# Turning the last query block's probabilities with 32x32 transposes and copies in the second attention of a two-layer trunk

## The chip, the cores and the metric

The kernel runs on one core of a Trainium2 chip. The metric is device time in microseconds (us) of one execution, the median of several. A core has a matrix engine (TensorE, PE in the profile; PEld are its weight loads), a vector engine (VectorE, DVE), an activation engine (ScalarE, ACT), a general engine (GpSimd, POOL) and an engine that issues transfers (SyncE, SP). They run side by side, each in its own order, and wait for one another at semaphores. Operands lie in SBUF, 128 partitions wide; TensorE writes to PSUM, which has eight banks of 128 x 512 float32 values.

## The reference

Two layers on 512 tokens of 1024 values. Each has an attention of 16 heads of 64 values and a gated MLP with 2816 inner values. The first layer's attention is stick-breaking; the second's, with which this document deals, is a softmax with a decay:

```python
z = jnp.einsum('bhqd,bhkd->bhqk', qb, kb).astype(jnp.float32) * scale
decay = cum[:, :, q0:k_end, None] - cum[:, :, None, :k_end]
logits = jnp.where(s_idx <= t_idx, z + decay, -jnp.inf)
p = jax.nn.softmax(logits, axis=-1)
outs.append(jnp.einsum('bhqk,bhkd->bhqd', p.astype(vb.dtype), vb))
```

Queries are taken in blocks of 128. Block 0 sees 128 keys, block 3 all 512. So a head has ten 128x128 blocks of probabilities, four of them in the last query block.

## The kernel before

Weights are loaded in tiles of 128x1024 and split on the chip into a rounded high half (ACT, L270) and a low half (POOL or DVE, L271); every product with a weight is three matmuls (`mm3`, L344 to L346). Three tiles of each half are kept, and a stream `ws` loads two tiles ahead of the one in use.

`attention` (L597) goes over the heads. For head h it issues the scores of query blocks 3, 2, 1, 0 (`scores`, L466, two matmuls each). In the second layer `fox` (L481) makes probabilities of each block: DVE adds the decay and finds the extreme value (L487), ACT takes the exponential and its sum (L490), DVE takes the reciprocal (L491) and scales (L492). The result `fx` has queries on partitions and keys along the row.

For the products with v the keys must be on partitions. This is done one head late: when head h has issued its block 2, `transposed` (L495) turns the probabilities of head h - 1. TensorE transposes 128x128 blocks into PSUM (tile `pa`, L504), and ACT evicts each bank to a tile `at` (L507). Three banks are used: key block 0 (512 columns, from four query blocks), key blocks 1 and 3 (384 and 128), and key block 2 (256). When both heads of a pair are turned, `weighted` (L510) multiplies them with v: for each key block and head one matmul of F32 operands (L516), into the pair's half of the 128 partitions of bank `po`, with the columns from that key block's first query to 511. The result is split into `oh` and `ol`, from which the output projection reads.

Between these steps, `fill` runs pieces of other work on TensorE: projections of later heads (`pqk`), values (`pv`), and towards the end the output projection of early heads. How many pieces each head gets is written in `UNITS`.

The orders of TensorE and of the transfer queue are those of the program. ACT, DVE and POOL are ordered by a planner, which goes by estimated costs; on the chip each then runs in that fixed order. Most 128x512 tiles (probabilities, `at`, v, queries and keys, `oh` and `ol`, some weights) share 44 slots of one pool; a new tile waits for a free one.

Of the kernel before, what the change touches and what calls it, by code (L numbers as in the profile page):

```python
# [8 lines left out]
F32 = mybir.dt.float32  # L9
F32R = mybir.dt.float32r  # L10
# [5 lines left out]
P = 128  # L16
D = 1024
S = 512
NT = S // P
ND = D // P  # L20
NH = 16
HD = 64
# [8 lines left out]
RES = 4  # L31
UNITS = [[10, 10, 10, 11, 10, 9, 10, 11, 9, 10, 10, 12, 8, 10, 4, 9, 6],
         [18, 12, 12, 12, 12, 12, 13, 12, 12, 12, 11, 9, 10, 10, 4, 9, 5]]
SH_A, SC_A, GT_A, SH_F, SC_F, GT_F = range(6)


@with_exitstack
def trunk(ctx, tc, x, c, w_mod, b_mod, g_mix_pre, g_mix_post, w_qkv, w_o, w_fg, b_fg,
          g_ffn_pre, g_ffn_post, w_gate, w_up, w_conv, b_conv, w_down, out):
    nc = tc.nc  # L40
    cst = ctx.enter_context(tc.tile_pool(name="cst", bufs=1))
# [5 lines left out]
    def nm(s):  # L47
        serial[0] += 1
        return f"{s}_{serial[0]}"

    def bank(s="b"):
        return pp.tile([P, 512], F32, tag="bank", name=nm(s), bufs=8)

    def slot(s, dt=F32R):
        return sb.tile([P, 512], dt, tag="slot", name=nm(s), bufs=NS)
# [17 lines left out]
    make_identity(nc, idn)  # L73
    onesf = cst.tile([P, P], F32, name="onesf")
    nc.vector.memset(onesf, 1.0)
    ones = cst.tile([P, P], F32R, name="ones")
    nc.vector.tensor_copy(ones, onesf)
    mhalf = cst.tile([P, 1], F32, name="mhalf")
    nc.vector.memset(mhalf, -0.5)
    mask = cst.tile([P, P], F32, name="mask")  # L80
# [188 lines left out]
    def split(hi, lo, src, engine=None):  # L269
        nc.scalar.copy(hi, src)  # L270
        (engine or nc.vector).tensor_tensor(lo, src, hi.bitcast(F32), op=ALU.subtract)  # L271
# [189 lines left out]
    def scores(l, hd, qb, q, k):  # L461
        n = (qb + 1) * P
        qs = slice(qb * P, n)
        ps = bank("ps")
        for i in range(2):
            nc.tensor.matmul(ps[:, :n], q[hd][:, qs], k[hd][i][:, :n], start=i == 0, stop=i == 1)  # L466
        return ps, n

    def stick(ps, n):


        bt = slot("bt", F32)
        om = slot("om", F32) if n > MULN else ps
        nc.gpsimd.memset(bt[:, n - 1 : n], 0.0)
        nc.scalar.activation(bt[:, : n - 1], ps[:, : n - 1], AF.Sigmoid)
        nc.scalar.activation(ps[:, :n], ps[:, :n], AF.Sigmoid, scale=-1.0)
        nc.vector.tensor_tensor_scan(om[:, :n][:, ::-1], ps[:, :n][:, ::-1], zid[:, S - n :][:, ::-1], 0.0, op0=ALU.mult, op1=ALU.add)
        (nc.gpsimd if n > MULN else nc.vector).tensor_tensor(bt[:, : n - 1], bt[:, : n - 1], om[:, 1:n], op=ALU.mult)
        return bt

    def fox(ps, qb, cum):  # L481

        n = (qb + 1) * P
        t = slot("fx", F32)[:, :n]
        e = t if n > MULN else ps[:, :n]
        m, s, r = tiny("mx"), tiny("sm"), tiny("rc")
        nc.vector.tensor_tensor_reduce(  # L487
            e.rearrange("p (b k) -> p b k", k=P), ps[:, :n].rearrange("p (b k) -> p b k", k=P), cum(qb),
            1.0, BIG, op0=ALU.add, op1=ALU.min, accum_out=m)
        nc.scalar.activation(e, e, AF.Exp, scale=-1.0, bias=m, accum_out=s)  # L490
        nc.vector.reciprocal(r, s)  # L491
        nc.vector.tensor_scalar(t, e, r, None, op0=ALU.mult)  # L492
        return t

    def transposed(probs):  # L495

        res = {}
        for kbs in ((0,), (1, 3), (2,)):
            ps, t, o = bank("pa"), slot("at", F32), 0
            for kb in kbs:  # L500
                n = (NT - kb) * P
                for qb in range(NT - 1, kb - 1, -1):
                    c = o + (qb - kb) * P
                    nc.tensor.transpose(ps[:, c : c + P], probs[qb][:, kb * P : (kb + 1) * P], idn)  # L504
                res[kb] = t[:, o : o + n]
                o += n
            nc.scalar.copy(t[:, :o], ps[:, :o])  # L507
        return res

    def weighted(p, vt, at, o):  # L510

        po = bank("po")
        for kb in range(NT):
            for hd in range(2):
                e = P * (p % 4) + HD * hd
                nc.tensor.matmul(po[HD * hd : HD * hd + HD, kb * P :], vt[p // 4, kb][:, e : e + HD], at[hd][kb],  # L516
                                 start=kb == 0, stop=kb == NT - 1, tile_position=(0, HD * hd))
        split(*o, po)

    def values(l, g, t, ht, vt):  # L520
# [76 lines left out]
    def attention(l, qk, vt, ot, filler, units, bgs):  # L597


        get = cums_of.get(l)  # L600
        late, ats, cums = None, {}, {}
        for h in range(NH + 1):
            p, hd = divmod(h, 2)
            done = [0, 0]

            def fill(n=1):
                done[0] += n
                u = (units[h] * min(done[0], 12) + 11) // 12 - done[1]
                done[1] += u
                filler.run(u)  # L610

            if h < NH and hd == 0:
                ot.append((slot("oh"), slot("ol")))
            if get and h < NH:
                for i in range(h, min(h + 2, NH)):
                    if i not in cums:
                        cums[i] = get(i)
            probs = {}
            for qb in range(NT - 1, -1, -1):
                if h < NH:  # L620
                    ps, n = scores(l, hd, qb, qk[p, 0], qk[p, 1])
                    probs[qb] = stick(ps, n) if l % 2 == 0 else fox(ps, qb, cums[h])
                    fill(2)
                if late and qb == 2:
                    ats[late[1] % 2] = transposed(late[0])
            fill(2 if h < NH else 10)
            if h % 2:
                for bg in bgs[:1]:
                    bg.step()
            if late and hd == 0:  # L630
                weighted(p - 1, vt, ats, ot[p - 1])
                ats = {}
            fill(12)
            late = (probs, h)
            if h:
                for bg in bgs[: 1 + (h > 1)]:
                    bg.step()
# [198 lines left out]
    for l in range(DEPTH):  # L836
# [42 lines left out]
        gens += [project(t, ps_) for ps_ in (range(3), range(3, 5)) for t in range(2)] + [project(2, range(3))]  # L879
        filler = Filler(gens)  # L880
        attention(l, qk, vt, ot, filler, UNITS[l], bgs)
        filler.finish()
        for bg in bgs:
# [130 lines left out]
```

## Time and profile before

| | |
|---|---|
| median of 3 runs | 1255.88 us (1254.57 to 1257.66) |
| profiled execution | 1257.99 us, its span 1256.2 us |
| second attention in it | scores of the first head at 670.2 us, last products with v at 855.8 us |
| granted clock of TensorE | 0.996 over the span |

The profile records each instruction with its engine, line and operands. A group line gives the engine, the operation, the tiles, the shape and count, then busy time and mean duration, then the idle time ahead of it and what ended that. Matmuls overlap, so their cost is the step from one start to the next and not their duration. A timeline line gives start, length, engine, line and what was run; instructions of one kind that follow each other are merged.

### The profile page before, as it was taken

Reading aid. Unit: us, or ns where it says so; the run is one execution under the profiler, and the core shown is the slowest. Engines: PE = TensorE matmul, PEld = TensorE weight load, DVE = VectorE, ACT = ScalarE, POOL = GpSimd, SP = SyncE. Lnnn points to the kernel's source line nnn. Section 1 sums busy time; section 2 is a strip of 40 time slices with the busy share of each in tenths; the row PEclk is TensorE's granted clock in tenths of the full one; section 3 lists DMA queues with packets and bytes.
Section 4 is the critical chain, followed back from the end, with each engine's and each line's share of the span. In section 5 each row is a group of like instructions: output and inputs, shape, how many; then the busy total and the mean of one; then the engine's idle time right before and its main releaser. Section 6 shows DMA issues by size and latency. Waiting matters only on the chain.

```text
span 1256.2 us, 16873 instructions
## 1 busy us (share of the span) xinstructions
PE 1234.3 (98%) x6300; PEld 1024.5 (82%) x6300; DVE 707.3 (56%) x1168; ACT 587.0 (47%) x1104; POOL 286.6 (23%) x348
## 2 busy tenths in 40 slices
PE   7999999999999999999999999999999999999997
PEld 5877877789888888888887888877988888888886
DVE  5667676277788988422364665564684444442233
ACT  7576666475333333222366565665733333331221
POOL 4775555510000000000216554452000000000000
PEclk9999999999999999999999999999999999999999
DMA  9737532225586677323405433333173333333231
GB/s 286 222 123 254 181 115 94 92 68 168 168 267 232 207 248 230 102 90 99 136 1 170 125 94 118 110 113 113 38 232 117 101 93 92 100 101 98 89 99 67
DMA packets 179400, 171.29 MB, mean 136 GB/s; under 512 B 7385, under 2 KB 152177, under 8 KB 179318
## 3 DMA queue, kind: packets, MB, share of 16 engines
q1 hardware_dynamic: 179142, 170.15, 43.6%
q8 instruction: 49, 0.80, 0.3%
q14 instruction: 33, 0.27, 0.1%
q10 hardware_dynamic: 176, 0.07, 0.0%
HBM read 168.01 MB, written 2.18 MB: 135 GB/s over the span
## 4 chain that ended last, share of the span: by engine, by line
PE 88%; DVE 4%; ACT 3%; issue 2%; DMA 1%; POOL 1%; SPq 0%; ACTq 0%; POOLq 0%; DVEq 0%
PE pgu L345 13%; PE pgu L346 13%; PE pgu L344 13%; PE pd L345 6%; PE pd L344 6%; PE pd L346 6%; PE pqk L344 4%; PE pqk L346 4%; PE pqk L345 4%; PE ps L466 3%; PE po L516 3%; PE pv L344 3%; PE pv L346 3%; PE pv L345 3%; PE pa L504 3%
## 5 line engine op out<-in xcount | busy, mean ns | idle before, releaser
L270 ACT CAST wh<-wf 128x1024 fp32r<-128x1024 f32 (+2 forms) x178 | 185.4, 1042 | 288.4 <-PE pgu L345 134.5
L345 PE MATMUL pgu<-htl,wh 128*128 128x512 f32 (+1 forms) x736 | 276.3, 375 | 0.6 <-DVE htl L406 0.6
L344 PE MATMUL pgu<-hth,wh 128*128 128x512 f32 (+1 forms) x736 | 276.4, 375 | 0.0
L346 PE MATMUL pgu<-hth,wl 128*128 128x512 f32 (+1 forms) x736 | 276.1, 375 | 0.0
L271 DVE TENSOR_TENSOR wl<-wf,wh 128x1024 fp32r<-128x1024 f32 x122 | 149.3, 1224 | 215.2 <-ACT wh L270 212.8
L345 PEld LDWEIGHTS pgu<-htl,wh 128*128 128x128 f32 x736 | 138.5, 188 | 26.1 <-DVE htl L406 1.0
L344 PEld LDWEIGHTS pgu<-hth,wh 128*128 128x128 f32 x736 | 138.5, 188 | 25.1
L346 PEld LDWEIGHTS pgu<-hth,wl 128*128 128x128 f32 x736 | 138.5, 188 | 24.6
L271 POOL TENSOR_TENSOR wl<-wf,wh 128x1024 fp32r<-128x1024 f32 (+3 forms) x56 | 129.8, 2321 | 108.6 <-ACT wh L270 106.4
L344 PE MATMUL pd<-wh,yh 128*128 128x512 f32 x288 | 112.0, 389 | 0.0
L345 PE MATMUL pd<-wl,yh 128*128 128x512 f32 x288 | 112.0, 389 | 0.0
L346 PE MATMUL pd<-wh,yl 128*128 128x512 f32 x288 | 112.0, 389 | 0.0
L357 POOL TENSOR_TENSOR r<-v,mhalf 128x1 f32<-128x1 f32 x32 | 17.6, 551 | 404.6 <-DVE v L353 404.6
L344 PE MATMUL pqk<-hth,wh 128*128 128x512 f32 (+1 forms) x240 | 94.1, 392 | 0.0
L346 PE MATMUL pqk<-hth,wl 128*128 128x512 f32 (+1 forms) x240 | 92.2, 384 | 0.4 <-POOL wl L271 0.4
L345 PE MATMUL pqk<-htl,wh 128*128 128x512 f32 (+1 forms) x240 | 92.1, 384 | 0.0
L926 ACT ACTIVATE cv<-cv 128x512 f32<-128x512 f32 x44 | 27.9, 633 | 133.8 <-DVE cv L925 133.8
L156 DVE SCALAR_TENSOR_TENSOR acc<-wm,csil,acc 128x1024 f32<-128x1024 f32 x52 | 66.7, 1282 | 10.9 <-DMA wm<-in_w_mod_dram 10.3
L344 PE MATMUL pv<-wh,hth 128*128 128x256 f32 (+1 forms) x224 | 68.8, 307 | 0.9 <-ACT hth L711 0.9
L346 PE MATMUL pv<-wh,htl 128*128 128x256 f32 (+1 forms) x224 | 67.3, 300 | 0.0
L345 PE MATMUL pv<-wl,hth 128*128 128x256 f32 (+1 forms) x224 | 67.2, 300 | 0.0
L344 PEld LDWEIGHTS pd<-wh,yh 128*128 128x128 f32 x288 | 54.1, 188 | 11.3
(202 smaller groups left out, 2221.8 us busy)
## 6 DMA issues: line engine op xcount, KB each, us to landing
wm<-in_w_mod_dram SPq DMA_DIRECT2D x72, 512.0 KB, 5.8
wf<-in_w_ffn_gate_dram SPq DMA_DIRECT2D x44, 512.0 KB, 3.9
wf<-in_w_ffn_up_dram SPq DMA_DIRECT2D x44, 512.0 KB, 4.0
wf<-in_w_ffn_down_dram SPq DMA_DIRECT2D x44, 512.0 KB, 3.5
wf<-in_w_qkv_dram SPq DMA_DIRECT2D x41, 512.0 KB, 4.0
wm<-in_w_mod_dram SPq DMA_DIRECT2D x48, 256.0 KB, 3.5
wf<-in_w_o_dram SPq DMA_DIRECT2D x16, 512.0 KB, 3.6
cum<-cumd SPq DMA_DIRECT2D x16, 512.0 KB, 4.7
```

Source lines behind the costliest of these rows:

```text
L156: nc.vector.scalar_tensor_tensor(acc, w, csil[:, d : d + 1], acc, op0=ALU.mult, op1=ALU.add)
L270: nc.scalar.copy(hi, src)
L271: (engine or nc.vector).tensor_tensor(lo, src, hi.bitcast(F32), op=ALU.subtract)
L344: nc.tensor.matmul(ps, ah, bh, start=first, stop=False)
L345: nc.tensor.matmul(ps, ah, bl, start=False, stop=False)
L346: nc.tensor.matmul(ps, al, bh, start=False, stop=last)
L357: nc.gpsimd.tensor_tensor(r, v, mhalf, op=ALU.pow)
L466: nc.tensor.matmul(ps[:, :n], q[hd][:, qs], k[hd][i][:, :n], start=i == 0, stop=i == 1)
L504: nc.tensor.transpose(ps[:, c : c + P], probs[qb][:, kb * P : (kb + 1) * P], idn)
L516: nc.tensor.matmul(po[HD * hd : HD * hd + HD, kb * P :], vt[p // 4, kb][:, e : e + HD], at[hd][kb], start=kb == 0, stop=kb == NT - 1, tile ...
L926: nc.scalar.activation(a, a, AF.Silu)
```

## The change

In the second layer alone (`l in (1,)`), the last query block of a head no longer goes through TensorE and PSUM. DVE turns the 128x512 tile in 32x32 blocks, each in its place (`tr`). Sixteen copies then bring the blocks to where a full transpose would have them: the copy (i, j) takes, from partitions 32i to 32i+31, the j-th 32 columns of all four key blocks, 128 values a partition, and writes them to partitions 32j to 32j+31 as the i-th 32 columns. `COPIES` gives them to the engines: five to DVE, six to POOL, five to ACT. The other six blocks are transposed by TensorE as before, into two banks (key blocks 0 and 2 with 384 and 128 columns, key block 1 with 256) with two evictions. `weighted` takes its columns in pieces: per head and key block one from the evicted tile and one of 128 columns from `own`, seven matmuls in place of four. An unused tile `ones` and its copy are removed.

```diff
+COPIES = [0, 1, 2, 0, 1, 2, 0, 1, 2, 0, 1, 2, 0, 1, 2, 1]
...
-    ones = cst.tile([P, P], F32R, name="ones")
-    nc.vector.tensor_copy(ones, onesf)
...
-    def transposed(probs):
-
-        res = {}
-        for kbs in ((0,), (1, 3), (2,)):
+    def transposed(probs, blocks):
+        res, nq = {kb: [] for kb in range(NT)}, NT - 1 if blocks else NT
+        if blocks:
+            t, own = slot("tr", F32), slot("at", F32)
+            nc.vector.transpose(t, probs[NT - 1])
+            src, dst = (x_.rearrange("p (k j c) -> p k j c", k=NT, c=32) for x_ in (t, own))
+            for n, (i, j) in enumerate((i, (i + k) % 4) for k in range(4) for i in range(4)):
+                copy = (nc.vector.tensor_copy, nc.gpsimd.tensor_copy, nc.scalar.copy)[COPIES[n]]
+                copy(dst[32 * j : 32 * j + 32, :, i, :], src[32 * i : 32 * i + 32, :, j, :])
+            for kb in range(NT):
+                res[kb].append((own[:, kb * P : (kb + 1) * P], nq * P))
+        for kbs in ((0, 2), (1,)) if blocks else ((0,), (1, 3), (2,)):
             ps, t, o = bank("pa"), slot("at", F32), 0
             for kb in kbs:
-                n = (NT - kb) * P
-                for qb in range(NT - 1, kb - 1, -1):
+                n = (nq - kb) * P
+                for qb in range(nq - 1, kb - 1, -1):
...
-                res[kb] = t[:, o : o + n]
+                res[kb].insert(0, (t[:, o : o + n], kb * P))
...
-            for hd in range(2):
-                e = P * (p % 4) + HD * hd
-                nc.tensor.matmul(po[HD * hd : HD * hd + HD, kb * P :], vt[p // 4, kb][:, e : e + HD], at[hd][kb],
-                                 start=kb == 0, stop=kb == NT - 1, tile_position=(0, HD * hd))
+            for n in range(len(at[0][kb])):
+                for hd in range(2):
+                    e = P * (p % 4) + HD * hd
+                    x_, c = at[hd][kb][n]
+                    nc.tensor.matmul(po[HD * hd : HD * hd + HD, c : c + x_.shape[-1]], vt[p // 4, kb][:, e : e + HD], x_,
+                                     start=kb + n == 0, stop=kb == NT - 1, tile_position=(0, HD * hd), skip_group_check=True)
...
-                    ats[late[1] % 2] = transposed(late[0])
+                    ats[late[1] % 2] = transposed(late[0], l in (1,))
```

## The prediction

> **What bounds the kernel now.** I read the page from the top, then the stage that the change touches, then single instructions in it.
>
> ```profile
> PE 1234.3 (98%) x6300; PEld 1024.5 (82%) x6300; DVE 707.3 (56%) x1168; ACT 587.0 (47%) x1104; POOL 286.6 (23%) x348
> PE 88%; DVE 4%; ACT 3%; issue 2%; DMA 1%; POOL 1%; SPq 0%; ACTq 0%; POOLq 0%; DVEq 0%
> ```
>
> TensorE is busy for 98% of the span and holds 88% of the chain of work that ended last. A microsecond taken off its queue is a microsecond off the span, as long as nothing else becomes late. The table of stretches for the second attention, without its first two heads and its very end, says the same more sharply (columns: stretch, length, then busy time of PE, PEld, DVE, ACT, POOL, granted clock, DMA share, GB/s):
>
> ```profile
> 690.00:858.00 168.00, 167.89 (x1026) 139.99 (x1024) 96.23 (x269) 98.92 (x236) 83.20 (x66) 1.00 0.36 110
> ```
>
> PE has 0.1 us of idle time in 168, at full clock; DVE is at 57%, ACT at 59%, POOL at 50%. The chain in order of time shows where that is least safe:
>
> ```profile
> 837.33 0.48 ACT at L507
> 837.85 0.68 PE ps L466 x4
> ```
>
> (Columns: start, length, engine, tile, line.) Here the path runs through ACT's eviction of transposed probabilities, up to the scores that start at 837.85: at this place PE has no lead over the other engines.
>
> **What leaves PE.** Four of ten transposes go, for each of 16 heads.
>
> ```profile
> L504 PE MATMUL pa<-zid,fx 128*128 128x128 f32 x160 | 20.1, 272 | 0.0
> 747.74 1.25 PE L504 MATMUL pa<-zid,fx 128*128 128x128 f32 x10
> 748.75 0.36 PE L466 MATMUL ps<-kh,qa 128*128 128x256 f32 x1
> ```
>
> The 272 ns is a latency, as matmuls overlap. The ten span 1.25 us, the last takes 0.27, so it starts at 748.72, and nine steps make 0.98 us: 0.109 us each. 64 x 0.109 = **7.0 us off** PE's queue. They are also 160 of the records of this stage, of which 96 should remain.
>
> **What the pieces add on PE.** Each product of F32 operands is two passes (16 matmuls for 8 calls). The columns stay 1280 per head and pass; the calls go from 8 to 14 a pair.
>
> ```profile
> 705.13 2.37 PE L516 MATMUL po<-at,v 128*64 128x512 f32 x16
> ...
> 705.61 0.14 PEld L516 LDWEIGHTS po<-at,v 128*64 128x64 f32 x2 [0.28 <-issue]
> 706.04 0.14 PEld L516 LDWEIGHTS po<-at,v 128*64 128x64 f32 x2 [0.28 <-issue]
> 706.36 0.14 PEld L516 LDWEIGHTS po<-at,v 128*64 128x64 f32 x2 [0.18 <-issue]
> 706.68 0.58 PEld L516 LDWEIGHTS po<-at,v 128*64 128x64 f32 x6 [0.18 <-issue]
> 706.90 0.60 PE L516 MATMUL po<-at,v 128*64 128x256 f32 x6
> ```
>
> Both heads step together. A step of 512 columns takes 0.43 us (705.61 to 706.04), of 384 0.32 (706.04 to 706.36, and again to 706.68), of 256 0.22 (706.68 to 706.90). The last six matmuls, 0.60 us with a last one of 0.27, hold one step of 256 and one of 128 in 0.33 us, so a 128 step takes 0.11. Before: 2 x (0.43 + 0.32 + 0.22 + 0.11) = 2.16. After: 2 x (0.32 + 0.22 + 5 x 0.11) = 2.18. That is 0.02 us a pair, **0.2 us** in eight. The bound above: should the loads of the weights (0.14 us) not hide behind such short matmuls, six more calls of two passes cost 12 x 0.14 = 1.68 us a pair, 13.4 us in all. I take 0.2, since the one 128 step in the trace shows its load hidden.
>
> [...]
>
> **PSUM.** A head takes two banks, not three. Once the trace shows what that is worth:
>
> ```profile
> 836.50 1.25 PE L504 MATMUL pa<-zid,fx 128*128 128x128 f32 x10
> 837.85 0.39 PE L466 MATMUL ps<-kh,qa 128*128 128x256 f32 x1
> ```
>
> The last transpose starts at 837.48 and the scores only at 837.85, behind the eviction in the chain above; at 748 us that step was 0.03. I take **0.3 us off**, between 0 and twice that.
>
> **What the other engines get.** The nearest rows for a 32x32 transpose of 128x512, and for copies of 128 columns:
>
> ```profile
> L227 DVE STREAM_TRANSPOSE tr<-acc 128x512 f32<-128x512 f32 x2 | 1.3, 678 | 0.0
> L77 DVE CAST ones<-onesf 128x128 fp32r<-128x128 f32 x1 | 0.2, 220 | 0.0
> L270 ACT CAST fgp<-fgw 128x128 fp32r<-128x128 f32 x1 | 0.3, 299 | 1.9 <-DMA fgw<-in_w_fg_dram 1.9
> L507 ACT COPY at<-pa 128x512 f32<-128x512 f32 x64 | 34.6, 588 | 10.5 <-PE pa L504 9.8
> L134 POOL COPY quad<-part 32x32 f32<-32x32 f32 x28 | 7.5, 267 | 187.4 <-DVE part L160 186.5
> L457 POOL TENSOR_SCALAR kh<-kh 64x512 fp32r<-64x512 f32 x32 | 20.3, 633 | 10.0 <-ACT kh L455 7.6
> ```
>
> Per head: DVE 0.68 + 5 x 0.22 = 1.78 us. ACT 5 x 0.30 less one eviction of 0.59 = 0.91. POOL 6 copies, each between 0.267 and 0.633; by columns 0.267 + 96/480 x 0.366 = 0.34, so 2.04. Sixteen heads in about 161 us then make DVE 96.2 + 28.5 = 125, ACT 98.9 + 14.6 = 114, POOL 83.2 + 32.6 = 116: 71 to 78% busy. No engine is full by this sum. Hidden under PE's filler, all of it costs nothing; without that cover it is PE waits. The removed cast to ones, 0.22 us before the first load matters, I cost at nothing, since the first products wait for loads from memory; without that cover it would be its own 0.22 us. A head takes four slots of the 44 (tr, own, two evictions) in place of three; tr is free again after sixteen copies, and the last block's own slot once it is turned. I cost that at nothing too; a late slot would hold up DVE's transpose, inside the margins below.
>
> The margins that cover it, odd heads first, since their products follow closest:
>
> ```profile
> 702.70 1.35 ACT L507 COPY at<-pa 128x512 f32<-128x512 f32 x3
> ...
> 775.39 1.35 ACT L507 COPY at<-pa 128x512 f32<-128x512 f32 x3
> 777.60 0.65 PE L516 MATMUL po<-at,v 128*64 128x512 f32 x2
> ...
> 798.83 1.35 ACT L507 COPY at<-pa 128x512 f32<-128x512 f32 x3
> 801.55 0.65 PE L516 MATMUL po<-at,v 128*64 128x512 f32 x2
> ...
> 838.78 0.37 ACT L507 COPY at<-pa 128x256 f32<-128x256 f32 x1
> 839.90 0.65 PE L516 MATMUL po<-at,v 128*64 128x512 f32 x2
> ```
>
> From the last eviction to the products there are 1.08, 0.86, 1.37 and 0.75 us for these four pairs; the other four have more. The new waits: ACT's and POOL's copies stand behind DVE's transpose, and the two engines are in order, so the next exponentials on ACT and the low halves of weights (2.4 us each) on POOL stand behind them; PE needs both. If only ACT's 0.91 us delays the evictions, PE waits some 0.2 us in all. If DVE's 1.78 comes on top, each tight pair waits 2.69 less its margin: 1.6 + 1.8 + 1.3 + 1.9, **6.7 us**. Between 0.2 and 6.7 I take **2 us**, nearer the low end, because the last block's probabilities are the first of a head to be finished and their turning can fill DVE's idle 43%.
>
> Sum: -7.0 + 0.2 - 0.3 + 2.0 = **-5.1 us**. The profiled execution took 1257.99 us, so 1252.9 in its terms; against the median 1255.88, 2.1 lower, that is **1250.8**.
>
> **Rivals.** *Margins eaten:* the waits come to 6.7 us and the sum is -0.4, 1255.5 us. For it speaks the path through ACT near 834 us, against it the four wide margins and the early start. *DVE becomes the bound, slower:*
>
> ```profile
> 690.61 2.68 DVE L492 TENSOR_SCALAR fx<-fx,rc 128x512 f32<-128x512 f32 x1
> 690.61 2.40 POOL L271 TENSOR_TENSOR wl<-wf,wh 128x1024 fp32r<-128x1024 f32 x1
> L492 DVE TENSOR_SCALAR fx<-fx,rc 128x512 f32<-128x512 f32 x15 | 16.1, 1070 | 0.1
> L387 DVE TENSOR_SCALAR xn<-xs,r 128x512 f32<-128x512 f32 x26 | 11.5, 483 | 8.2 <-POOL r L357 8.2
> L491 DVE RECIPROCAL rc<-sm 128x1 f32<-128x1 f32 x60 | 9.8, 163 | 38.0 <-ACT fx L490 21.3 <-ACT ps L490 16.6
> ```
>
> The same scaling takes 0.48 us where POOL is quiet, 1.07 here in the mean, and 2.68 beside a POOL instruction of 2.40: it waits POOL out, 0.59 us on average. The five copies of a head could meet the same, and POOL gets 40% more work. With 125 us of DVE work and half of the 38 us that it now waits for exponentials it has 144; 80 copies that wait 0.3 us each fill the old 168, and from there the change is slower. At 0.5 us each, 184: 16 us over, 1272. Against it: a head's copies can run back to back, so that the first pays for all. [...] *Weight loads show:* 13.4 us in place of 0.2, a sum of +8.1, 1264.0 us; the one row that exists speaks against it.
>
> **How the numbers follow.** Chances: the forecast 0.57, margins eaten 0.27, DVE as bound 0.13, loads 0.03. A measurement of this kernel tells a change from none from about 0.3%, 3.8 us. The forecast lies beyond that on the fast side (its own range 1248.5 to 1252), margins eaten within it, the last two on the slow side: 0.57 / 0.27 / 0.16. The range runs from 1247.5 (no wait at all, a little more from PSUM) to 1260 (all margins eaten and one PE wait of half a microsecond in half of the heads); above it lie the two slow cases.
>
> **What would show it.** The transposes of this attention should count 96, and the products 224 with steps of 0.11 us for 128 columns: right steps one and two. PE's idle time between 690 and 850 us should be about 2 us, next to the products of odd heads. It is wrong if the copies on DVE take well over 0.22 us in the mean, if PE idles 5 us or more in the stage, or if consecutive 128 steps cost 0.2 us.

## The result, and the profile after

The changed kernel is slower: 1268.44 us (median of five runs, 1266.70 to 1268.89) against 1256.46 for the kernel before, a ratio of 1.0089 with a 95% interval of 1.0075 to 1.0103. That is 12 us more, and more than the 0.3% that a measurement of this kernel can tell. The forecast was 5 us less, and its range ended at 1260.

The top of the profile's page, of the kernel after (engine, busy time and share of the span, instructions; then the shares of the chain that ended last):

```profile
span 1265.9 us, 17226 instructions
PE 1232.5 (97%) x6332; PEld 1023.6 (81%) x6332; DVE 739.0 (58%) x1263; ACT 603.0 (48%) x1168; POOL 314.8 (25%) x444
PE 81%; DVE 7%; ACT 6%; issue 2%; DMA 2%; POOL 1%; SPq 0%; DVEq 0%; POOLq 0%; ACTq 0%
```

TensorE's share of the chain fell from 88% to 81%, and DVE's and ACT's rose from 7% together to 13%. So TensorE now waits for them somewhere. The table of stretches of the kernel after says where (the columns are those of the prediction; the first row is the same 168 us of the second attention, the second the whole stage from the first head's scores to the last product with v, the last two are 3.41 us each within it):

```profile
690.00:858.00 168.00, 156.80 (x996) 133.00 (x995) 121.77 (x347) 109.21 (x283) 105.64 (x150) 0.98 0.35 105
668.85:867.65 198.80, 186.21 (x1146) 156.25 (x1147) 136.92 (x389) 125.98 (x318) 124.39 (x173) 0.98 0.40 120
706.26:709.67 3.41, 2.74 (x16) 1.81 (x18) 2.43 (x11) 2.12 (x8) 0.64 (x3) 0.50 0.00 0
849.62:853.03 3.41, 3.41 (x23) 2.70 (x20) 1.43 (x6) 1.55 (x5) 0.00 (x0) 0.50 0.05 13
```

The same stage of the kernel before:

```profile
670.23:857.87 187.64, 187.06 (x1114) 155.69 (x1115) 105.01 (x293) 109.76 (x254) 95.93 (x77) 1.00 0.42 127
```

The stage grew by 198.80 - 187.64 = 11.2 us. It starts 1.4 us earlier here (in the profiles of all kernels it starts between 667.8 and 670.7 us), and from its end to the end of the kernel both profiles take 398 us. PE's idle time in it grew from 0.58 us to 12.59, while its busy time fell by only 0.85. That is less than the 6.8 us of work taken off it, because it ran two stretches of 3.41 us at half clock. It was busy for 2.74 and 3.41 us in them. At the end of the second the step from a product of 512 columns to the next took 0.43 us (852.42 to 852.85), behind it 0.23 (853.17 to 853.40), so by estimate half of the busy time, 1.4 and 1.7 us, is what the low clock cost. Some 2.9 us of busy time are left over and stand in no single row; the ends of matmuls are modelled, and short gaps between products that wait for their pieces can be counted as busy.

The loss isn't spread evenly. Taken from one head's first scores to the next head's, nine of sixteen iterations became shorter, by 0.38 to 0.45 us each, as forecast (0.44). Seven became longer: those of head 14 by 5.0 us, 2 by 4.4, 13 by 2.8, 4 by 1.6, and three by 0.2 to 0.5. The view of what PE waited for names the same few places (kernel after, 690 to 872 us; total us, times, longest):

```profile
PE po L528 <- ACT at L517: 4.8, 2, 2.7
PE po L345 <- POOL wl L271: 2.9, 1, 2.9
PE ps L466 <- DVE mx L487: 1.7, 1, 1.7
PE po L528 <- POOL at L505: 1.6, 1, 1.6
```

Together 11.0 us in five waits. L528 are the products with v, L517 the evictions of the blocks that TensorE still transposes, L505 the copies; `wl` is the low half of an output weight.

**The first of these waits**, in the timeline of the kernel after (start, length, engine, line, what was run; the bracket is the idle time ahead and what ended it):

```profile
689.51 0.62 DVE L492 TENSOR_SCALAR fx<-fx,rc 128x512 f32<-128x512 f32 x1
...
701.68 2.15 DVE L492 TENSOR_SCALAR fx<-fx,rc 128x384 f32<-128x384 f32 x1
701.02 2.59 POOL L271 TENSOR_TENSOR wl<-wf,wh 128x1024 fp32r<-128x1024 f32 x1
703.75 0.70 DVE L501 STREAM_TRANSPOSE tr<-fx 128x512 f32<-128x512 f32 x1
704.48 1.52 ACT L505 COPY at<-tr 32x128 f32<-32x128 f32 x5 [1.83 <-DVE tr L501]
706.28 0.87 ACT L517 COPY at<-pa 128x512 f32<-128x512 f32 x2
706.93 3.72 PE L528 MATMUL po<-at,v 128*64 128x384 f32 x26 [2.66 <-ACT at L517]
```

Read it from the top. At 690.13 the last block's probabilities of head 1 are finished. They are turned at 703.75, because in DVE's order the turning stands in the middle of the iteration of head 2, behind the scaling of that head's blocks. The scaling directly ahead of it takes 2.15 us, beside a low half on POOL of 2.59. ACT's five copies wait 1.83 us for that turning, and then take 1.52. Behind them stand the evictions, which needed nothing but PE. PE waits 2.66 us for the last of them, and then runs at half clock until 709.67.

**The copies themselves** in the groups of the kernel after (stretch 690 to 868 us; busy us and mean ns of one stand behind the first bar):

```profile
L505 DVE COPY at<-tr 32x128 f32<-32x128 f32 x80 | 31.0, 387 | 1.1
```

and in the view of tile `tr` (shortest, median and longest duration in ns):

```profile
L505 POOL COPY at<-tr x96: 281/285/597, 693.8 to 864.8; 32x128 f32<-32x128 f32 x96
L505 ACT COPY at<-tr x80: 293/296/299, 690.8 to 863.3; 32x128 f32<-32x128 f32 x80
L505 DVE COPY at<-tr x80: 215/312/2334, 692.5 to 864.2; 32x128 f32<-32x128 f32 x80
L501 DVE STREAM_TRANSPOSE tr<-fx x16: 692/699/711, 690.1 to 861.4; 128x512 f32<-128x512 f32 x16
```

POOL's and ACT's copies are as cheap as forecast, or cheaper. DVE's take 215 ns at best and up to 2334. The timeline shows five of them without a low half on POOL beside them, and five with one:

```profile
811.61 0.21 DVE L505 COPY at<-tr 32x128 f32<-32x128 f32 x1
812.19 1.18 DVE L505 COPY at<-tr 32x128 f32<-32x128 f32 x4
...
834.56 2.35 POOL L271 TENSOR_TENSOR wl<-wf,wh 128x1024 fp32r<-128x1024 f32 x1
834.85 3.97 DVE L505 COPY at<-tr 32x128 f32<-32x128 f32 x5
836.96 0.50 PE L345 MATMUL po<-wl,oh 128*128 128x512 f32 x1 [2.88 <-POOL wl L271]
```

First 0.21 + 1.18 us, then, beside POOL's low half of 2.35 us, 3.97. The last row is the second of the waits above: PE stood 2.88 us for that same low half, so POOL too was late.

### The profile page after: what moved, and what is told of

It reads as the page before. It is cut to its first block, busy times and chain, and to the rows that moved or that the text cites. A ratio compares the mean times of both kernels' runs of the same rounds, so it can differ in the third digit from the quotient of the medians.

```text
span 1265.9 us, 17226 instructions
## 1 busy us (share of the span) xinstructions
PE 1232.5 (97%) x6332; PEld 1023.6 (81%) x6332; DVE 739.0 (58%) x1263; ACT 603.0 (48%) x1168; POOL 314.8 (25%) x444
## 4 chain that ended last, share of the span: by engine, by line
PE 81%; DVE 7%; ACT 6%; issue 2%; DMA 2%; POOL 1%; SPq 0%; DVEq 0%; POOLq 0%; ACTq 0%
PE pgu L345 13%; PE pgu L346 13%; PE pgu L344 13%; PE pd L345 6%; PE pd L344 6%; PE pd L346 6%; PE pqk L344 3%; PE po L528 3%; PE pqk L345 3%; PE pqk L346 3%; PE pv L344 2%; PE ps L466 2%; PE pv L346 2%; PE pv L345 2%; PE pa L514 2%
```

## The experiments

Two theories stood at the start. **Order:** the turning and the copies are late because they are written in the middle of the next head's iteration, and what stands behind them in the queues of ACT, POOL and DVE, evictions and weight halves, is late with them. **Ports** (the name that the expectations use): DVE's copies wait for POOL's instructions, as the scaling at 690.61 in the prediction seems to (2.68 us beside one of 2.40), and DVE falls behind. The rivals of the prediction, pieces whose weight loads show and a full engine, were tried too. Ratios are against the kernel before, run on the same chip, with 95% intervals; a diff shows a kernel against the changed one unless it says otherwise.

**The pieces alone.** The last block goes through TensorE again, in a bank and an eviction of its own; the products stay in pieces.

```diff
-            t, own = slot("tr", F32), slot("at", F32)
-            nc.vector.transpose(t, probs[NT - 1])
...
+            ps, own = bank("pa"), slot("at", F32)
+            for kb in range(NT):
+                nc.tensor.transpose(ps[:, kb * P : (kb + 1) * P], probs[NT - 1][:, kb * P : (kb + 1) * P], idn)
+            nc.scalar.copy(own, ps)
```

> The products with v go in seven pieces a head as in the change, but TensorE transposes the last query block too (into its own bank, one eviction of 512), and no copies run. Theory 'pieces' (the short products with their weight loads cost PE time): 4 to 13 us over before, 1260 to 1270 us. Theories 'queues' (turning and copies stand ahead of what PE waits for) and 'ports' (copies and scalings on DVE wait for POOL): within 0.3% of before, 1253 to 1260 us, steps of 0.11 us for 128 columns.

1257.80 us, 1.0010 [1.0000, 1.0019]. Its chain has the products of a pair in one row (start, length, tile, line, count):

```profile
754.76 2.32 PE po L526 x28
```

The kernel before has there

```profile
753.76 2.31 PE po L516 x16
```

Twelve more matmuls cost 0.01 us a pair. The pieces aren't the cause, and the weight loads of 0.14 us stay hidden behind steps of 0.11.

**The copies left out.** DVE turns the 32x32 blocks straight into `own`; the sixteen copies are gone.

```diff
-            t, own = slot("tr", F32), slot("at", F32)
-            nc.vector.transpose(t, probs[NT - 1])
...
+            own = slot("at", F32)
+            nc.vector.transpose(own, probs[NT - 1])
```

> DVE's transpose writes straight to the tile that the products read; the sixteen copies are left out, so the last block's probabilities lie in other places than they should. All theories that blame the copies: the gain on PE is there, about 6 to 7 us under before, 1249 to 1251 us. If DVE's transpose itself or its wait for the scaling makes PE wait: 1254 us or more.

1251.52 us, 0.9961 [0.9949, 0.9972]: 4.9 us faster than before. So most of the 6.8 us do come off PE's queue, and the copies with what they make late cost 0.0089 + 0.0039 of the time, some 16 us. Between 690 and 858 us PE idles 1.75 us, where the kernel before has 0.11, in one wait:

```profile
836.94 0.33 PE L466 MATMUL ps<-kh,qa 128*128 128x128 f32 x1 [1.75 <-DVE mx L487]
```

Even without a copy PE isn't always the last to come. The changed kernel has the same wait, before the same scores and as long (1.7 in the list above), so this one of the five isn't due to the copies.

**Turning and copies early.** They are written at the end of the head's own iteration, ahead of its last filler, and not in the middle of the next.

```diff
+            own = turned(probs[NT - 1]) if l == 1 and h < NH else None
...
-            late = (probs, h)
+            late = (probs, h, own)
```

> The same turning and copies with the same shares of the engines, but written into the program at the end of the head's own iteration, after the products of the pair before, in place of the middle of the next one, just ahead of the evictions. Theory 'queues': most waits of PE go, 1249 to 1256 us. Theory 'ports': the copies on DVE meet the same POOL instructions wherever they stand, the cost stays: 1262 to 1268 us.

1263.66 us, 1.0056 [1.0041, 1.0071]. It gives back 0.0033 of 0.0089. The place in the program is a part of the cause, and not the whole. In its profile the waits of 1.5 to 2.7 us for evictions, copies and scores are gone; those that are left are under 1 us, but for one, for a low half at the late place:

```profile
833.74 0.79 PE L345 MATMUL po<-wl,oh 128*128 128x512 f32 x1 [5.17 <-POOL wl L271]
```

**Only the middle heads.** The change in heads 4 to 11 alone:

```diff
-                    ats[late[1] % 2] = transposed(late[0], l in (1,))
+                    ats[late[1] % 2] = transposed(late[0], l == 1 and 4 <= late[1] < 12)
```

> The change in heads 4 to 11 alone, the stretch in which the changed kernel's profile shows next to no wait of PE. If each head there gains its 0.44 us as the two traces say: 3 to 4 us under before, 1252 to 1254 us. If the gain is given back later, as by a wait that the saved time only moves: 1256 us.

1258.66 us, 1.0011 [1.0001, 1.0020]. Its profile has one wait of over half a microsecond in heads 1 to 15, of 2.45 us for a low half at 831.68, and the mean granted clock from 690 to 858 us is 0.99, where the kernel before has 1.00: most of the gain was given back at one place, behind heads 10 and 11, which the last experiments take up.

**No copies on DVE** (eight each on POOL and ACT):

```diff
-COPIES = [0, 1, 2, 0, 1, 2, 0, 1, 2, 0, 1, 2, 0, 1, 2, 1]
+COPIES = [1, 2] * 8
```

> Sixteen copies as before, eight on POOL and eight on ACT, none on DVE; DVE keeps its transpose. Theory 'ports' (copies on DVE wait for POOL, which holds up the rest): most of the loss goes, 1250 to 1258 us. Theory 'queues' (whatever stands behind the turning on any engine is late): ACT and POOL carry more, so no better than the change, 1264 to 1275 us.

1275.77 us, 1.0155 [1.0129, 1.0181]: slower still. **Ports** alone would have made it faster. PE waits for ACT's evictions more often (690 to 872 us in this kernel):

```profile
PE po L528 <- ACT at L517: 6.8, 5, 2.4
```

**No copies on ACT** (eight each on DVE and POOL):

```diff
-COPIES = [0, 1, 2, 0, 1, 2, 0, 1, 2, 0, 1, 2, 0, 1, 2, 1]
+COPIES = [0, 1] * 8
```

> Eight copies on DVE and eight on POOL, none on ACT, so that nothing on ACT waits for DVE's transpose and its evictions and casts of weights come as early as PE lets them. Theory 'queues', with ACT's queue as the one that decides: 1255 to 1261 us. Theory 'ports': more copies meet POOL, 1268 us or more.

1276.65 us, 1.0161 [1.0144, 1.0178]. The evictions now stand behind no copy, and PE waits for the copies themselves:

```profile
PE po L528 <- DVE at L505: 5.3, 3, 3.6
PE po L528 <- POOL at L505: 4.5, 4, 2.9
```

So ACT's queue isn't the one that decides. Whether DVE or ACT is relieved, the other two become late by more.

**DVE's copies in another form.** A sum over an axis of one value copies it:

```diff
+    def one_port(d, s):
+        nc.vector.tensor_reduce(d, s.unsqueeze(3), axis=AX.X, op=ALU.add)
...
-                copy = (nc.vector.tensor_copy, nc.gpsimd.tensor_copy, nc.scalar.copy)[COPIES[n]]
+                copy = (one_port, nc.gpsimd.tensor_copy, nc.scalar.copy)[COPIES[n]]
```

> [...] Theory 'ports': a DVE copy no longer waits for POOL, the longest copy drops from 2.3 us to about 0.3 us, and the time falls by half of the loss or more, below 1262 us. Theory 'queues': each copy is a little longer in the quiet case, the scalings still wait for POOL, and the time stays at 1264 to 1270 us.

1263.84 us, 1.0056 [1.0040, 1.0072]. The row of these copies (shortest, median, longest in ns):

```profile
L496 DVE TENSOR_REDUCE at<-tr x80: 266/278/283, 692.0 to 857.4; 32x128 f32<-32x128 f32 x80
```

No copy on DVE waits any more: 278 ns in the middle and 283 at most, where the plain ones took 215 at best and up to 2334. (In the kernel before, sums over pieces of a row took 660 ns for 512 columns and 1214 for 1024, at L228 and L160. The same slope gives some 0.24 us for 128, an estimate: a little more than a plain copy at its best.) That takes back 0.0033, 4 us. **Ports** holds for DVE's copies, and is also a part.

**Only the turning early**, the copies in their old place:

```diff
-            t, own = slot("tr", F32), slot("at", F32)
-            nc.vector.transpose(t, probs[NT - 1])
+            t, own = probs[NT], slot("at", F32)
...
+            if l == 1 and h < NH:
+                probs[NT] = slot("tr", F32)
+                nc.vector.transpose(probs[NT], probs[NT - 1])
```

> DVE's transpose alone is written at the end of the head's own iteration; the sixteen copies stay where they are, just ahead of the evictions. If the copies on ACT and POOL are late because the transpose stands behind a scaling that waits for POOL: they no longer wait for it and the time falls to 1255 to 1261 us. If the copies' own time in the queues is what counts: 1264 to 1268 us.

1266.29 us, 1.0076 [1.0061, 1.0091]. The interval overlaps that of the change. That ACT's copies wait for the turning is a small part of it; the copies are what has to move.

**The evictions first.** TensorE's transposes and their evictions are written ahead of the turning and the copies, within the same function.

```diff
-        if blocks:
-            t, own = slot("tr", F32), slot("at", F32)
-            nc.vector.transpose(t, probs[NT - 1])
...
             nc.scalar.copy(t[:, :o], ps[:, :o])
+        if blocks:
+            t, own = slot("tr", F32), slot("at", F32)
+            nc.vector.transpose(t, probs[NT - 1])
...
```

> The change with TensorE's six transposes and their evictions written ahead of the turning and the copies. If ACT's copies cost time because they stand ahead of the evictions that PE waits for: 1258 to 1264 us. If it is the copies themselves that come too late for the products: no better than the change, 1267 us or more.

1262.88 us, 1.0046 [1.0030, 1.0061]. It gives back 0.0043, more than the early place or the other form, though the intervals overlap. The products no longer wait for an eviction, but for the copies behind it:

```profile
PE po L528 <- POOL at L515: 6.2, 4, 2.5
```

**Early, and in the other form**, all sixteen heads (both edits shown above):

> Both remedies in all sixteen heads. If each takes its half of the loss, 1253 to 1259 us; if the late output weights near the end decide, 1260 us or more, with one PE wait of several microseconds there.

1258.01 us, 1.0005 [0.9996, 1.0014]. The two parts add up: 0.0033 and 0.0033 were expected to leave 0.0023, and 0.0005 is left. The stretch of 168 us, and in the timeline the largest wait that remains:

```profile
690.00:858.00 168.00, 161.83 (x1043) 137.85 (x1043) 125.27 (x363) 115.04 (x298) 110.50 (x157) 1.00 0.36 111
```

```profile
831.17 0.50 PE L345 MATMUL po<-wl,oh 128*128 128x512 f32 x1 [2.26 <-POOL wl L271]
```

DVE is busier than in the changed kernel (75% of the stretch against 72%), ACT and POOL too, and yet the kernel is 10 us faster. Busy shares don't explain the loss. The longest wait that remains is the one for a low half at the same late place; besides it there are five of 0.2 to 1.0 us between 690 and 858 us, for DVE and ACT.

**The change in heads 4 to 9 alone**, otherwise as it is:

```diff
+                    ats[late[1] % 2] = transposed(late[0], l == 1 and 4 <= late[1] < 10)
```

> The change in heads 4 to 9 alone, with COPIES as in the change. If the gain of heads 4 to 11 was given back at one place, where the copies of heads 10 and 11 delay the casts and low halves of the first output weights: that wait is gone and six heads gain 0.44 us each, 1253.5 to 1255 us where before takes 1256.5. If the time saved is given back by the late weights whatever delays them: within 0.1% of before.

1254.41 us, 0.9980 [0.9971, 0.9989]. Six heads at 0.44 us are 2.6; measured are 2.5 of 1257.03, with an interval of 1.4 to 3.6. In its profile five of the six iterations that hold the turned blocks are 0.43 to 0.45 us shorter than before. The last is 0.41 longer: there the products of heads 8 and 9 take 3.2 us in place of 2.3, one head's ahead of the other's. Where nothing is late the change gives what was forecast.

**Heads 10 and 11 alone:**

```diff
+                    ats[late[1] % 2] = transposed(late[0], l == 1 and 10 <= late[1] < 12)
```

> The change as it is in heads 10 and 11 alone. If these two delay the casts and low halves of the output weights: the PE wait of 2 us or more in head 13 is there, with a stretch of half the clock behind it, and the time is 1.5 to 4 us over before in spite of 0.9 us saved. If that wait needed the time saved by the heads ahead of them: within 1 us of before, no such wait.

1258.64 us, 1.0014 [1.0005, 1.0023]. Two heads turn a gain of 0.9 us into a loss of 1.8. The chain of it, in the timeline of this kernel:

```profile
813.37 2.02 DVE L492 TENSOR_SCALAR fx<-fx,rc 128x512 f32<-128x512 f32 x1
815.31 0.70 DVE L501 STREAM_TRANSPOSE tr<-fx 128x512 f32<-128x512 f32 x1
816.05 1.53 ACT L505 COPY at<-tr 32x128 f32<-32x128 f32 x5 [1.84 <-DVE rc L491]
817.60 0.86 ACT L517 COPY at<-pa 128x512 f32<-128x512 f32 x2
819.25 1.03 ACT L270 CAST wh<-wf 128x1024 fp32r<-128x1024 f32 x1
820.41 2.39 POOL L271 TENSOR_TENSOR wl<-wf,wh 128x1024 fp32r<-128x1024 f32 x1 [1.53 <-issue]
823.21 0.42 SPq L582 DMA_DIRECT2D cum<-cumd  x1
827.93 1.44 POOL L584 TENSOR_TENSOR cum<-cum,mask 128x256 f32<-128x256 f32 x2 [5.13 <-DVE mx L487]
829.31 2.35 POOL L271 TENSOR_TENSOR wl<-wf,wh 128x1024 fp32r<-128x1024 f32 x1
831.72 0.80 PE L345 MATMUL po<-wl,oh 128*128 128x512 f32 x1 [2.31 <-POOL wl L271]
```

A turning behind a slow scaling, copies behind the turning, evictions behind the copies, then the cast of a weight's high half on ACT and its low half on POOL. Only when that has let go of its buffer the transfer queue of SP goes on, with a weight's load and behind it a load of `cum`. POOL, in order, does `cum` and only then the next low half, for which PE waits 2.31 us. (The row of `cum` names DVE as what ended POOL's wait. By the trace the load of `cum` landed at 827.79, 0.14 us ahead of that row, and in the kernel before it landed 0.13 us ahead.) In the kernel before, the same evictions, cast, low half and the first product with it are

```profile
817.57 1.35 ACT L507 COPY at<-pa 128x512 f32<-128x512 f32 x3 [0.47 <-PE pa L504]
...
818.98 1.05 ACT L270 CAST wh<-wf 128x1024 fp32r<-128x1024 f32 x1
...
829.12 2.40 POOL L271 TENSOR_TENSOR wl<-wf,wh 128x1024 fp32r<-128x1024 f32 x1
...
832.51 0.39 PE L345 MATMUL po<-wl,oh 128*128 128x512 f32 x1
```

The stage begins at 670.23 us there and here at

```profile
667.84 0.50 PE L466 MATMUL ps<-kh,qa 128*128 128x512 f32 x1 [1.44 <-POOL kh L457]
```

so the times are compared from these starts. The evictions begin 147.3 us into the stage before and 149.8 with the change, 2.4 later; the cast 148.8 and 151.4; the low half 158.9 and 161.5, 2.6 later. A delay of the evictions on ACT goes through the cast, the buffer, SP's queue and `cum` without getting smaller, over 12 us. Before, the low half was ready at 831.52, 1.0 us ahead of its product. PE comes 0.7 us earlier with the change (829.41 or 161.6 us into the stage, against 162.3). 2.6 + 0.7 - 1.0 = 2.3 us, the wait. After it, PE ran at half clock:

```profile
832.00:834.00 2.00, 2.00 (x5) 1.54 (x6) 0.00 (x0) 0.98 (x2) 1.84 (x3) 0.50 0.56 133
```

**Early, in the other form, ten heads.** Heads 0 to 9, and heads 2 to 11; the diff is against the version with both edits in all sixteen heads, and the second kernel has `2 <= h < 12` in the same place:

```diff
-            own = turned(probs[NT - 1]) if l == 1 and h < NH else None
+            own = turned(probs[NT - 1]) if l == 1 and h < 10 else None
```

> Both remedies, in heads 0 to 9 alone: the turning stands at the end of the head's own iteration, and DVE's copies are the slower ones that do not wait for POOL. If the two causes are the place in the queues and the ports, ten heads gain 0.44 us each less a microsecond of small waits: 1252 to 1254.5 us, under both kernels. If the other engines' added time counts wherever it stands: 1256 us or more.

> Early turning and copies that do not wait for POOL, in heads 2 to 11: without the first two heads, where that version lost a microsecond at the start, and without the last four. If heads 10 and 11 delay the output weights only through the late turning of the change: ten clean heads, 4.4 us under before, 1251.5 to 1253.5 us. If their copies delay the weights wherever they stand: a PE wait of 2 us or more in head 13, 1255 to 1258 us.

1254.75 us, 0.9981 [0.9971, 0.9990], and 1254.73 us, 0.9983 [0.9974, 0.9992]. Both are faster than the kernel before, by 2.4 and 2.1 us, and like the version with heads 4 to 9 they beat both kernels; but ten heads at 0.44 should give 4.4. In the profile of the second all ten iterations that hold a turned block are shorter by 0.43 to 0.45 us, and the wait for a low half at the late place is gone, although heads 10 and 11 are turned. One wait has come behind them (680 to 872 us in this kernel):

```profile
PE ps L466 <- ACT at L524: 0.9, 1, 0.9
```

A wait of 0.9 us for a low half at 684.50 stands ahead of the first copy, and the kernel before has it too, at 683.95 with 0.4, so it isn't the copies'. In the profile of the first, eight iterations are shorter by 0.43 to 0.45 us, and a new wait of 0.9 us stands at 692.11, behind the turning of head 0. With four heads more than in the version of six, nothing more is won that the medians show; the interval of the second, 1.0 to 3.3 us, ends below 4.4. The waits make up a part of what is missing, and no run took them away one by one.

## Why the prediction was wrong

**PE's queue** was right. The transposes count 96, and an undisturbed head gains 0.38 to 0.45 us, where 0.44 was worked out. Heads 4 to 9 alone give 2.5 us of 2.6.

**The pieces** were right: 0.2 us forecast, no more than a fraction of it seen in the steps (2.32 us a pair against 2.31), and 1.0010 for the kernel with the pieces alone, which also has an eviction and a bank of its own. The rival of weight loads that show falls.

**PSUM**'s 0.3 us can't be told apart in any run.

**The durations** were right in sum, and wrong in one part. Forecast for the 168 us were 125 us on DVE, 114 on ACT and 116 on POOL; measured are 121.8, 109.2 and 105.6, in a stretch that holds somewhat less of the work. But one DVE copy took 387 ns in the mean where 220 was the nearest row.

**The waits** are the step that failed. "Between 0.2 and 6.7 I take 2 us, nearer the low end, because the last block's probabilities are the first of a head to be finished and their turning can fill DVE's idle 43%." In the forecast's own sum, with -7.0 + 0.2 - 0.3 and the measured +12.0, this term is 19 us. The copies with all that they delay cost some 16 of it. Two of the three signs of being wrong that the prediction named came: DVE's copies at 387 ns, and 11.2 us of idle time on PE in the 168. Three things were missing in that step:

- *The turning doesn't fill idle time.* In the order that the engines run it stands about where the program writes it, in the middle of the next head's iteration, behind that head's scaling, and its copies ahead of ACT's evictions. That the data were ready 13.6 us earlier (690.13 to 703.75) changes nothing. Turning and copies written early give back 0.0033; the turning alone gives little, so what counts is the copies' place.
- *The margins counted were those from evictions to products.* The wait at 836.96 is one for a low half of a weight, and in the kernel with heads 10 and 11 alone the way to it was followed: cast, low half, buffer, transfer queue, low half. The first line of that step says that exponentials and low halves stand behind the copies, and then the sum leaves them out. Where it could be measured, the margin was 1.0 us and the delay 2.6.
- *A PE wait costs more than its length* where the clock halves after it: 1.4 and 1.7 us, 3.1 us of the stage's time here.

**DVE as the bound** gave 1272 us, the nearest of the forecasts, by a mechanism that is only half right. DVE was 72% busy, and its copies waited 0.17 us in the mean (387 less 220), below the 0.3 at which that rival starts to be slower. Taking the copies off DVE made it worse. But DVE's wait for POOL is in the rows: five plain copies took 3.97 us beside a low half and 1.39 without one, and the slowest plain copy took 2334 ns. The slowest in the other form took 283, and that form was worth 0.0033.

Early copies and the other form together take the change from 1.0089 to 1.0005, and leaving out the heads whose late chain runs through the weights makes it a gain of 0.2%. Not settled is to which of their small waits the ten-head versions lose the rest of their 4.4 us.

## What to carry to other kernels

Work moved off a full engine is free only if it has a place in the order of each engine that takes it; look at what stands directly behind it in each queue, and not at the busy shares. For every chain that goes through those queues, weights and transfers too, set the delay that the new work makes against the margin with which the chain now arrives. Write work that is ready early where it is ready, and don't put plain VectorE copies beside long GpSimd instructions: five of them took 3.97 us here beside one of 2.35, and 1.39 without it.

## What the runs showed of the hardware

- In the profiles of the two kernels PE's granted clock was 1.00, but for stretches of 3.41 us at 0.50, and 0.50 at the very end (from 1262.63 us with the change, from 1253.36 before). The stretches start at 218.15, 706.26 and 849.62 us with the change, at 21.15 and 219.12 before. Within a profile these starts are 488.11, 143.36 and 197.97 us apart, which is 143, 42 and 58 times 3.413. In the second attention of the changed kernel, PE had idled longer in the 3.41 us just ahead of each of its two stretches than in any other length of 3.41 us in step with them. Four of these lengths (the second and third follow each other):

```profile
702.85:706.26 3.41, 1.42 (x8) 0.62 (x6) 3.37 (x6) 1.72 (x6) 3.06 (x7) 1.00 0.01 3
832.55:835.96 3.41, 1.53 (x7) 0.94 (x5) 3.37 (x5) 3.08 (x9) 2.77 (x3) 1.00 0.00 0
835.96:839.37 3.41, 2.41 (x11) 1.99 (x12) 3.30 (x7) 0.02 (x1) 3.10 (x6) 1.00 0.37 108
846.21:849.62 3.41, 1.26 (x13) 0.74 (x14) 2.56 (x14) 2.90 (x9) 2.27 (x7) 1.00 0.74 243
```

  PE idled 1.99 us in the first, 1.88 in the second and 2.15 in the last, and what came behind them ran at 0.50, 1.00 and 0.50. The wait of 2.88 us that ended at 836.96 lay with 1.88 us ahead of 835.96 and with 1.00 behind it, and cost no clock. Nor did the wait of 2.26 us in the kernel with both remedies, where the clock was 1.00 from 829 to 834.50 us. The wait of 2.31 with heads 10 and 11 alone did cost it: the clock was 0.90 in the mean from 829 to 832 and from 834 to 838, and 0.50 between. By estimate that is half clock from 831.4 to 834.8, with 2.0 us of the wait ahead of it. A limit for other stages doesn't follow: at the start of the kernel before, 1.45 us of idle time between 17.73 and 21.15 stood ahead of a stretch at 0.50.
- A copy as a sum over an axis of one value costs DVE 278 ns, where the plain one takes 215 at best. It didn't wait for POOL: the slowest of 80 took 283 ns, where the slowest plain one took 2334.
- DVE's 32x32 transposes of 128x512 took 692 to 711 ns, all sixteen of them in the changed kernel, also those with POOL at work beside them, as at 703.75 (POOL from 703.70 on for 1.30 us). They didn't wait as the plain copies did.
